# Moving column factors and low halves between VectorE, ScalarE and GpSimd in a hybrid decoder layer

## The chip, the cores and the metric

The kernel runs on one core of a Trainium2 chip. The metric is the device time of one launch in microseconds (us), as the median over runs of the same kernel. Engines: TensorE (PE; PEld is its weight load), VectorE (DVE), ScalarE (ACT), GpSimd (POOL), SyncE (SP, which issues most DMAs).

## The reference

One decoder layer over 2048 tokens of 1024 channels, in float32. The lines that matter:

```python
a = _rmsnorm(h, g_pre_mix[l])
u = jnp.einsum("bsd,dc->bsc", a, w_in[l])          # conv value, conv gate, q, k, v: 5 x 512 columns
conv_out = _conformer_conv(c_val, c_gate, ...)     # GLU, causal depthwise conv of width 31, LayerNorm, swish
attn_out = _stick_breaking(q, k, v)                # 8 heads of 64, no softmax: running products of sigmoids
attn_out = _rmsnorm(attn_out, attn_norm_g[l])
mixed = jnp.concatenate([conv_out, attn_out], axis=-1)
y = jnp.einsum("bsc,cd->bsd", mixed, w_out[l])
h = h + _rmsnorm(y, g_post_mix[l])
f_in = _rmsnorm(h, g_pre_ffn[l])
f = silu(f_in @ w_gate) * (f_in @ w_up) @ w_down   # 2816 hidden channels
h = h + _rmsnorm(f, g_post_ffn[l])
```

`_rmsnorm(x, g)` is `x * rsqrt(mean(x*x) + eps) * g`: a factor for each row (token) and a factor for each channel.

## The kernel before, in words

Tokens are worked on in NG = 4 groups of G = 512 (g = 0 to 3), each of TT = 4 tiles of 128 rows; channels lie in KT = 8 tiles of 128. Activations stand as columns, that is with channels on the partitions and the 512 tokens of a group along the free dimension, so that they can be the moving operand of a matmul with weights as the stationary one.

All large products are made in three parts. An operand x is split in a high half H, its value rounded to the type fp32r, and a low half L = x - H. A product is then L*W_H + H*W_H + H*W_L, three matmuls in fp32r. So each operand costs one pass that rounds (always on ScalarE) and one that subtracts (VectorE or GpSimd). `dense` issues the three matmuls for each channel tile of the input projection (L600, L602, L604), `outproj` those of the output projection (L1043 to L1045), `matmul` (L1117) those of the feed-forward part.

The columns of the first group come from rows that are scaled and turned by TensorE (`scaled`, `to_col`). Those of groups 1 to 3 come from a copy of x that the host has laid out turned: `stats(T)` makes the row factor `rstd1` for 128 tokens; `turned(T)` spreads the four factors of a group over all partitions (`rb`), loads two channel tiles of the turned x into a tile `xcol`, and multiplies each by `rb` on GpSimd (L713). Later `prep(g)` walks over the eight channel tiles: ScalarE multiplies by the channel factor `gpm` and rounds to H (L739), VectorE multiplies by `gpm` again and subtracts H to get L (L740). `xtiles` gives the four tiles that hold H and L of a group, from a pool with two buffers for each kind, which `mixed` shares.

`inproj(g)` computes the 20 blocks of 128 columns for the group. Beside it run three side strands: `attn` (scores L910 and L911, sigmoid `om` L913, running product L916 or L918 on VectorE, transposes L936, their high half TH on ScalarE and low half TL on VectorE in `split` L592 and L593, values L941 and L942), `taps` (the convolution as 31 multiply-adds of 128x512 for each channel tile on VectorE, L826, then a normalization), and `sums` (sums of weight blocks for the feed-forward part on GpSimd, L1201; that part uses Strassen's seven products).

When the conv part (part 0) or the attention part (part 1) of a group is ready, `mixed(g, part)` splits its four channel tiles: H on ScalarE (L873), L on VectorE (L874). `outproj(g, part)` multiplies with w_out, whose own low halves GpSimd makes the first time (`load_w`, L558) and which are read back from memory later. `residual(T)` normalizes the result, adds x and stores the row `hd[T]` together with its factor `rstd2`. `hscaled(T)` loads such a row again and multiplies it by `rstd2` on VectorE (L720); `ffn_in` turns it into columns for the feed-forward part. The rows of the last group are kept and scaled on ScalarE (L1087). `c11` and `p4` are feed-forward products that already run within the mixer; `five` and the loop after it (products b and dps) make the rest.

Two things set the order of the work. The list `PLAN` with the lines `ATTN`, `TAPS` and `SUMS` says in which order the program's instructions are written down: it interleaves main stages and side strands. Then `Graph` takes all instructions up to the end of the last `outproj`, with a cost for each (`cost`, from engine, kind, width, and whether an operand is in PSUM), places them in time under their dependencies and buffers in up to 13 passes forward and backward, and keeps the shortest; `in_order` fixes for each engine the order found. Engines then run in that order and wait for semaphores where data comes from elsewhere. So when an operation changes engine or kind, the order of the mixer on all engines is found anew. After that point the order is the one in which the program is written, in part pinned with `keep_in_program_order`.

Of the kernel before, what the change touches and what calls it, by code (L numbers as in the profile page):

```python
# [10 lines left out]
F32 = mybir.dt.float32  # L11
F32R = mybir.dt.float32r
BF16 = mybir.dt.bfloat16
AF = mybir.ActivationFunctionType
ALU = mybir.AluOpType
# [466 lines left out]
def layer_kernel(ctx: ExitStack, tc: tile.TileContext, x, xT, g_pre_mix, w_in, conv_w, conv_b, ln_g, ln_b,  # L482
                 attn_g, w_out, g_post_mix, g_pre_ffn, w_gate, w_up, w_down, g_post_ffn, out):
    nc = tc.nc
# [13 lines left out]
    rstd2 = cp.tile([P, S // P], F32, name="rstd2")  # L498
# [4 lines left out]
    def const(pool, name, src, shape):  # L503
        t = pool.tile(shape, F32, name=name)
        waiting.append((t, src))
        return t
# [7 lines left out]
    gpm = const(cp, "gpm", g_pre_mix, [P, KT])  # L514

    def bank(name):
        return mm.tile([P, G], F32, tag="mm", name=name)
# [4 lines left out]
    def row(name):  # L522
        return rp.tile([P, D], F32, tag="row", name=name, bufs=4)
# [50 lines left out]
    class Weights:  # L574
# [9 lines left out]
        def next(self):  # L584
            while len(self.tiles) < min(self.n + 1 + self.ahead, len(self.srcs)):
                self.tiles.append(self.load(self.srcs[len(self.tiles)]))
            self.n += 1
            return self.tiles[self.n - 1]
# [109 lines left out]
    def turned(T):  # L698

        g, kp = divmod(T, TT)  # L700
        if kp == 0:
            assert need(*[("stats", g * TT + t) for t in range(TT)])()
            ps = bank("tps")
            for t in range(TT):
                q = g * TT + t
                nc.tensor.transpose(ps[:, t * P:(t + 1) * P], rstd1[:, q:q + 1].to_broadcast([P, P]), id32)
            rb = fup.tile([P, G], F32, tag="rb", name="rb")
            nc.scalar.activation(rb, ps, AF.Copy)
            rbs[g] = rb
        r = row("xcol").rearrange("p (i t) -> p i t", i=2)  # L710
        nc.sync.dma_start(r, xT[g, kp])
        for i in range(2):
            nc.gpsimd.tensor_tensor(r[:, i, :], r[:, i, :], rbs[g], ALU.mult)  # L713
        rows["x", T] = r

    def hscaled(T):
        assert ("h", T) in done
        r = row("hrow")
        nc.sync.dma_start(r, hd[T])
        nc.vector.tensor_scalar(r, r, rstd2[:, T:T + 1], None, ALU.mult)  # L720
        rows["h", T] = r

    def cols(rs, tiles, g, banks=bank):
        for k in range(KT):
            to_col(rs, k, *tiles, g, banks)
            yield 1

    def prep(g):
        xs[g] = xtiles()
        if g == 0:  # L730
            idle = cycle(("z", "at"))
            yield from cols([rows[t] for t in range(TT)], xs[g], gpm,
                            lambda name: pp.tile([P, G], F32, tag=next(idle), name=name))
            return
        Hs, Ls = xs[g]
        for k in range(KT):
            r = rows["x", g * TT + k // 2][:, k % 2, :]
            H = Hs[k // 4][:, k % 4, :]
            nc.scalar.activation(H, r, AF.Copy, scale=gpm[:, k:k + 1])  # L739
            nc.vector.scalar_tensor_tensor(Ls[k // 4][:, k % 4, :], r, gpm[:, k:k + 1], H.bitcast(F32), ALU.mult,  # L740
                                           ALU.subtract)
            yield 1

    def xtiles():
        Hs, Ls = [], []
        for hf in range(2):
            H = xp.tile([P, 4, G], F32R, tag="xH", name="xH", bufs=2)
            L = xp.tile([P, 4, G], F32R, tag="xL", name="xL", bufs=2)
            Hs.append(H)
            Ls.append(L)  # L750
        return Hs, Ls
# [115 lines left out]
    def mixed(g, part, tiles=xtile):  # L867

        yield need(("attn" if part else "conv", g))
        H, L = mc[g, part] = tiles()  # L870
        ms = [ma[g, p] if part else conv[g][:, p, :] for p in range(CB)]
        for k in range(CB):
            nc.scalar.activation(H[:, k, :], ms[k], AF.Copy)  # L873
            nc.vector.tensor_tensor(L[:, k, :], ms[k], H[:, k, :].bitcast(F32), ALU.subtract)  # L874
        if part:
            done.add(("mix", g))
        yield 1
# [406 lines left out]
    def chain(gens):  # L1284
        for gen in gens:
# [3 lines left out]
    taps_s = Side(chain(taps(g) for g in range(NG)), 1 / (NG * (CB * CW + 3 * (TAPLAG + LAG * TT))), ("taps", "conv"))  # L1289
    sums_s = Side(sums(), 1 / (10 * HF))  # L1290
    fns = {"prep": (prep, 8), "qkv": (lambda g: inproj(g, qkv), 12), "gv": (lambda g: inproj(g, gv), 8),
           "in": (lambda g: inproj(g, both), 20),
           "mixc": (lambda g: mixed(g, 0), 1), "outc": (lambda g: outproj(g, 0), 4),
           "mixa": (lambda g: mixed(g, 1), 1), "outa": (lambda g: outproj(g, 1), 4), "fprep": (ffn_in, 8), "c11": (c11, 2 * HF),
           "p4": (p4, 2 * HF)}
    def each(fn):
        def gen(g):
            for t in range(TT):
                fn(g * TT + t)
                yield 1  # L1300
        return gen

    fns["residual"], fns["hscaled"] = (each(residual), TT), (each(hscaled), TT)
    quick = {"scaled": scaled, "stats": stats, "turned": turned, "hscaled": hscaled, "residual": residual,
             "tprep": tprep}
    sides = ((attn_s, ATTN), (taps_s, TAPS), (sums_s, SUMS))
# [32 lines left out]
    with ExitStack() as E:  # L1339
# [13 lines left out]
        for _ in mixed(NG - 1, 1, lambda: operand(*e[0:2])):  # L1353
            pass
# [264 lines left out]
        r = [(R[0], f"t{i}") for i in range(4)]  # L1619
# [77 lines left out]
        for i, (g, n, j) in enumerate(slots):  # L1697
# [9 lines left out]
            if n in (5, 3) and j < TT:  # L1707
                T, r = (TB + j, hrows[j]) if n == 5 else (TA + j, hrows[TT + j])
# [96 lines left out]
```

## Time and profile before

| | |
|---|---|
| median of 3 runs | 2428.36 us (2428.14 to 2428.55) |
| the profiled execution | 2429.93 us, span of its instructions 2428.1 us |
| granted TensorE clock in it, mean | 0.995 |
| PE, DVE, ACT, POOL busy | 2353.6, 1766.3, 1163.8, 1196.0 us |
| the mixer | from 0 to about 1410 us, the rest of the feed-forward part after it |

In the rows of the profile, L and a number is the line of the kernel, then the engine, the operation, the tile written and the tiles read, the shapes, and the count. Times in rows of groups are busy us in all and the mean ns of one, then the idle time of that engine just before them and who ended it. A row of a timeline begins with the start and the duration in us. "PE x L600 <- DVE y L593: 2.9, 5, 1.4" means that PE, before its instructions of line 600 that write x, stood idle for 2.9 us in all, 5 times, 1.4 us at the longest, until VectorE's line 593 had written y.

### The profile page before, as it was taken

To read this page: it belongs to the slowest core of one execution; us is meant where nothing else is said; L and a number is where in the kernel's file an instruction comes from. 1 tells how busy PE (TensorE), PEld (TensorE's weight loads), DVE (VectorE), ACT (ScalarE), POOL (GpSimd) and SP (SyncE) were. 2 spreads that over 40 slices of the span, in tenths; PEclk is the share of its full clock that TensorE was granted. 3 is DMA by queue.
4 is the path that set the end of the run, shared out by engine and by line. 5 is a ranking of instruction groups with operands and counts; after the bars stand their busy time and mean duration, and the time that the engine had idled before them with its cause. 6 is when DMAs were issued, how large, how long until landed. Compare 5 with 4: busy or idle time off the path is not lost. (4 is left out here: it accounts for less than half of the span.)

```text
span 2428.1 us, 33643 instructions
## 1 busy us (share of the span) xinstructions
PE 2353.6 (97%) x11156; PEld 1929.4 (79%) x11156; DVE 1766.3 (73%) x2177; ACT 1163.8 (48%) x2078; POOL 1196.0 (49%) x994
## 2 busy tenths in 40 slices
PE   7999999999999999999999998999999999999998
PEld 5778888788888878887888877777888888887886
DVE  6897899999997799847832357667666664556557
ACT  4346555574555455455564553333232235454443
POOL 5462336422424333428700057755766665467656
PEclk9999999999999999999999999999999999999999
DMA  9888876998688899987897769878888877668765
GB/s 315 266 263 313 259 248 216 308 314 266 223 300 310 264 321 341 314 290 257 266 341 244 272 227 335 310 257 277 295 286 267 271 253 257 196 191 280 236 191 178
DMA packets 283790, 656.67 MB, mean 270 GB/s; under 512 B 34912, under 2 KB 35424, under 8 KB 283616
## 3 DMA queue, kind: packets, MB, share of 16 engines
q1 hardware_dynamic: 267776, 625.68, 77.3%
q10 hardware_dynamic: 15840, 28.84, 3.1%
q8 instruction: 88, 1.44, 0.2%
q14 instruction: 86, 0.70, 0.1%
HBM read 460.40 MB, written 193.99 MB: 270 GB/s over the span
## 5 line engine op out<-in xcount | busy, mean ns | idle before, releaser
L826 DVE SCALAR_TENSOR_TENSOR cv<-glu,cw,cv 128x512 f32<-128x512 f32 x464 | 346.9, 748 | 6.2
L1411 POOL TENSOR_TENSOR wL<-raw,wH 128x512 fp32r<-128x512 f32 x176 | 254.8, 1470 | 194.5 <-ACT wH L1410 163.1
L1642 DVE TENSOR_TENSOR xL__20078<-t__20080,xH__20077 128x512 fp32r<-128x512 f32 x154 | 200.4, 1306 | 159.9 <-ACT xH__20077 L1641 159.8
L1640 POOL TENSOR_TENSOR xL__20076<-t__20079,xH__20075 128x512 fp32r<-128x512 f32 x154 | 212.7, 1388 | 153.6 <-ACT xH__20075 L1639 145.4
L593 DVE TENSOR_TENSOR TL<-at,TH 128x512 fp32r<-128x512 f32 (+1 forms) x320 | 189.5, 601 | 127.7 <-ACT TH L592 117.3
L600 PE MATMUL inps<-xH,wL 128*128 128x512 f32 x640 | 259.4, 406 | 9.9 <-ACT sg L770 8.8
L604 PE MATMUL inps<-xL,wH 128*128 128x512 f32 x640 | 255.7, 401 | 0.6 <-DVE xL L740 0.6
L602 PE MATMUL inps<-xH,wH 128*128 128x512 f32 x640 | 256.3, 401 | 0.0
L1117 PE MATMUL dps<-xL__20076,xH__20077 128*128 128x512 f32 x616 | 240.1, 390 | 2.8 <-POOL xL__20076 L1640 2.8
L1117 PE MATMUL dps<-xH__20075,xL__20078 128*128 128x512 f32 x616 | 240.1, 390 | 2.5 <-DVE xL__20078 L1642 2.1
L1117 PE MATMUL dps<-xH__20075,xH__20077 128*128 128x512 f32 x616 | 239.8, 389 | 0.0
L554 ACT ACTIVATE wH<-raw 128x1024 fp32r<-128x1024 f32 x156 | 165.4, 1061 | 139.9 <-PE inps L604 62.9
L592 ACT ACTIVATE TH<-at 128x512 fp32r<-128x512 f32 (+1 forms) x320 | 168.8, 537 | 130.2 <-PE at L936 113.7
L913 ACT ACTIVATE om<-z 128x512 f32<-128x512 f32 (+2 forms) x320 | 168.8, 542 | 89.3 <-PE z L911 87.8
L1639 ACT ACTIVATE xH__20075<-t__20079 128x512 fp32r<-128x512 f32 x154 | 97.3, 632 | 217.2 <-POOL xL__20076 L1640 121.2
L558 POOL TENSOR_TENSOR wL<-raw,wH 128x1024 fp32r<-128x1024 f32 x50 | 123.1, 2467 | 155.9 <-ACT wH L554 119.3
L936 PE MATMUL at<-idr,om 128*128 128x128 f32 x1088 | 185.4, 273 | 7.2 <-DVE TL L593 2.7
L1410 ACT ACTIVATE wH<-raw 128x512 fp32r<-128x512 f32 x176 | 101.2, 623 | 167.7 <-PE b L1117 49.8
L936 PEld LDWEIGHTS at<-idr,om 128*128 128x128 f32 x1088 | 136.8, 140 | 48.0 <-DVE TL L593 6.3
L1201 POOL TENSOR_TENSOR sum<-sum 128x512 f32<-128x512 f32 x88 | 124.6, 1416 | 100.2 <-DMA sum<-in_w_up_dram 40.3
L918 DVE TENSOR_TENSOR_SCAN om<-om,z 128x512 f32<-128x512 f32 x124 | 156.8, 1271 | 8.5 <-ACT om L913 8.2
L600 PEld LDWEIGHTS inps<-xH,wL 128*128 128x128 f32 x640 | 121.7, 190 | 34.5 <-ACT sg L770 5.8
(296 smaller groups left out, 6103.9 us busy)
## 6 DMA issues: line engine op xcount, KB each, us to landing
wL<-wL SPq DMA_DIRECT2D x156, 512.0 KB, 5.3
raw<-in_w_in_dram SPq DMA_DIRECT2D x80, 512.0 KB, 5.8
t__20080<-u SPq DMA_DIRECT2D x154, 256.0 KB, 2.8
c<-c ACTq DMA_DIRECT2D x88, 256.0 KB, 5.3
t__20079<-wd SPq DMA_DIRECT2D x88, 256.0 KB, 2.9
K<-kd SPq DMA_DIRECT2D x80, 256.0 KB, 4.9
V<-vd SPq DMA_DIRECT2D x80, 256.0 KB, 5.0
u<-accf SPq DMA_DIRECT2D x22, 768.0 KB, 4.6
```

The lines of the kernel that those rows point to most:

```text
L592: nc.scalar.activation(H, ps, AF.Copy)
L593: nc.vector.tensor_tensor(L, ps, H.bitcast(F32), ALU.subtract)
L600: nc.tensor.matmul(ps, WL[:, kc], aH[t](k), start=k == 0, stop=False)
L602: nc.tensor.matmul(ps, WH[:, kc], aH[t](k), start=False, stop=False)
L604: nc.tensor.matmul(ps, WH[:, kc], aL[t](k), start=False, stop=k == KT - 1)
L826: nc.vector.scalar_tensor_tensor(to, gl[c][:, k:k + G], cw[:, c, k:k + 1], a, ALU.mult, ALU.add)
L913: nc.scalar.activation(om[:, 0:w], z[:, 0:w], AF.Sigmoid, scale=-0.125)
L936: nc.tensor.transpose(pt[:, j * P:(j + 1) * P], u["A"][j][:, b * P:(b + 1) * P], id32)
L1117: return nc.tensor.matmul(ps, a, b, skip_group_check=True, **flags)
L1411: nc.gpsimd.tensor_tensor(l, t, f32(h), sub)
L1640: nc.gpsimd.tensor_tensor(WL, w, f32(WH), sub)
L1642: nc.vector.tensor_tensor(UL, t, f32(UH), sub)
```

## The change

Four edits, all before the feed-forward part's second half:

- `turned`: before GpSimd multiplies a channel tile by the row factors, a new pass on ScalarE multiplies it by the channel factor `gpm`, in place (24 passes of 128x512).
- `prep`, groups 1 to 3: the pass that rounds to H no longer multiplies, and L is a plain subtraction on GpSimd in place of the multiply-and-subtract on VectorE (24 times).
- `mixed`: L is subtracted on GpSimd in place of VectorE (32 times, all four groups and both parts).
- `hscaled`: the row of 128x1024 is scaled on ScalarE in place of VectorE (12 times).

```diff
@@ turned
         for i in range(2):
+            nc.scalar.activation(r[:, i, :], r[:, i, :], AF.Copy, scale=gpm[:, 2 * kp + i:2 * kp + i + 1])
             nc.gpsimd.tensor_tensor(r[:, i, :], r[:, i, :], rbs[g], ALU.mult)
@@ hscaled
-        nc.vector.tensor_scalar(r, r, rstd2[:, T:T + 1], None, ALU.mult)
+        nc.scalar.activation(r, r, AF.Copy, scale=rstd2[:, T:T + 1])
@@ prep
-            nc.scalar.activation(H, r, AF.Copy, scale=gpm[:, k:k + 1])
-            nc.vector.scalar_tensor_tensor(Ls[k // 4][:, k % 4, :], r, gpm[:, k:k + 1], H.bitcast(F32), ALU.mult,
-                                           ALU.subtract)
+            nc.scalar.activation(H, r, AF.Copy)
+            nc.gpsimd.tensor_tensor(Ls[k // 4][:, k % 4, :], r, H.bitcast(F32), ALU.subtract)
@@ mixed
-            nc.vector.tensor_tensor(L[:, k, :], ms[k], H[:, k, :].bitcast(F32), ALU.subtract)
+            nc.gpsimd.tensor_tensor(L[:, k, :], ms[k], H[:, k, :].bitcast(F32), ALU.subtract)
```

## The prediction

> **What bounds the kernel now.** I read the page first: the busy shares, the slices, the chain.
>
> ```profile
> span 2428.1 us, 33643 instructions
> PE 2353.6 (97%) x11156; PEld 1929.4 (79%) x11156; DVE 1766.3 (73%) x2177; ACT 1163.8 (48%) x2078; POOL 1196.0 (49%) x994
> PE   7999999999999999999999998999999999999998
> DVE  6897899999997799847832357667666664556557
> POOL 5462336422424333428700057755766665467656
> ```
>
> TensorE is covered nearly everywhere, so only its gaps can be won. VectorE has two lives: in the first 16 slices (971 us, most of the mixer) it stands mostly at 8 or 9 tenths, in the last 16 (from 1457 us, which this change does not edit) at 4 to 7. GpSimd is loose in both, with crowded slices. Next the same by stretches (busy time of PE, PEld, DVE, ACT, POOL, each with its count, then clock, DMA share, GB/s):
>
> ```profile
> 150.00:1000.00 850.00, 833.80 (x4265) 684.57 (x4264) 785.13 (x1081) 472.64 (x850) 321.48 (x322) 1.00 0.86 284
> 1000.00:1390.00 390.00, 386.16 (x1890) 316.16 (x1889) 207.71 (x241) 215.81 (x378) 134.07 (x104) 1.00 0.83 280
> 400.00:440.00 40.00, 39.04 (x181) 30.93 (x180) 39.93 (x53) 18.84 (x30) 29.14 (x26) 1.00 0.76 268
> ```
>
> From 150 to 1000 us PE stands idle 850 - 833.8 = 16.2 us (1.9%) with VectorE busy 92.4%; from 1000 to 1390 us 3.84 us (1.0%) with VectorE at 53%. A busy PE can still be held up, because its matmuls overlap. That shows in the mean of one 128x512 matmul: here the groups of the first stretch, and last the same shape in the down projection (1700 to 2400 us), where VectorE is loose:
>
> ```profile
> L600 PE MATMUL inps<-xH,wL 128*128 128x512 f32 x503 | 202.7, 403 | 3.8 <-ACT sg L770 2.8 <-DVE glu L775 0.5 <-DVE big L1048 0.2
> L604 PE MATMUL inps<-xL,wH 128*128 128x512 f32 x503 | 200.8, 400 | 0.6 <-DVE xL L740 0.6
> L602 PE MATMUL inps<-xH,wH 128*128 128x512 f32 x503 | 200.7, 399 | 0.0
> L910 PE MATMUL z<-K,QL 128*128 128x512 f32 x156 | 65.3, 418 | 1.3 <-DVE om L918 1.3
> L942 PE MATMUL o<-TL,V 128*128 128x512 f32 x155 | 64.4, 415 | 2.2 <-DVE TL L593 2.2
> L1117 PE MATMUL dps<-xH__20075,xL__20078 128*128 128x512 f32 x591 | 230.2, 390 | 1.9 <-DVE xL__20078 L1642 1.5 <-ACT t__20082 L1713 0.4
> ```
>
> The excess over 390 ns is (13 + 10 + 9) x 503 + 28 x 156 + 25 x 155 ns = 24.3 us. It bounds from above what the busy time hides, since part of it is only the change between matmul shapes. So at most 16.2 + 24.3 = 40.5 us are to be won in the stretch where VectorE is full. Who is named for PE's visible gaps from 150 to 1390 us (us in all, times, longest; four largest rows of VectorE, and the largest of ScalarE):
>
> ```profile
> PE o L942 <- DVE TL L593: 2.9, 5, 1.4
> PE inps L600 <- ACT sg L770: 2.8, 2, 1.9
> PE ops L1043 <- DVE vt L593: 1.6, 2, 1.1
> ...
> PE at L936 <- DVE TL L593: 1.6, 3, 0.6
> PE z L910 <- DVE om L918: 1.3, 4, 0.5
> ```
>
> VectorE leads with 7.4 us in these four rows, but no single wait is long: the kernel is bound by PE, with VectorE close behind.
>
> **The change part by part.** What leaves VectorE (the first 1400 us; count, busy us and mean ns of one behind the bar, the idle time before them last), and the four late pieces of the last mixed rows:
>
> ```profile
> L740 DVE SCALAR_TENSOR_TENSOR xL<-xcol,gpm,xH 128x512 fp32r<-128x512 f32 x24 | 22.1, 926 | 0.0
> L874 DVE TENSOR_TENSOR xL<-acc,xH 128x512 fp32r<-128x512 f32 x16 | 12.8, 823 | 5.8 <-ACT xH L873 5.8
> L720 DVE TENSOR_SCALAR hrow<-hrow,rstd 128x1024 f32<-128x1024 f32 x12 | 12.8, 1074 | 0.0
> L874 DVE TENSOR_TENSOR xL<-ma,xH 128x512 fp32r<-128x512 f32 x12 | 11.0, 934 | 1.2 <-PE at L936 1.0 <-ACT xH L873 0.2
> L874 DVE TENSOR_TENSOR e__15143<-ma,e__15142 x4: 683/684/693, 1393.2 to 1398.3; 128x512 fp32r<-128x512 f32 x4
> ```
>
> That is 22.1 + 12.8 + 12.8 + 11.0 + 4 x 0.684 = 61.4 us. Some 44 us of it fall between 150 and 1000 us: all of L740, 16 of the 28 L874 (13.9), 8 of the 12 L720 (8.6). What the other engines do instead is priced by these rows:
>
> ```profile
> L713 POOL TENSOR_TENSOR xcol<-xcol,rb 128x512 f32<-128x512 f32 x24 | 33.4, 1421 | 5.4 <-ACT rb L708 5.4
> L571 POOL TENSOR_TENSOR wL<-raw,wH 128x512 fp32r<-128x512 f32 x22 | 35.1, 1599 | 11.7 <-ACT wH L570 8.6 <-PE z L911 3.2
> L739 ACT ACTIVATE xH<-xcol,gpm 128x512 fp32r<-128x512 f32 x24 | 16.4, 724 | 6.4 <-POOL xcol L713 4.5 <-PE ops L1045 1.3 <-PE inps L602 0.6
> L873 ACT ACTIVATE xH<-acc 128x512 fp32r<-128x512 f32 x16 | 9.3, 626 | 4.4 <-PE c L1117 4.3
> L541 ACT ACTIVATE junk<-big 128x1024 f32<-128x1024 f32 x24 | 25.3, 1057 | 22.6 <-POOL big L1080 16.8 <-DVE big L1048 3.9 <-DVE xL L740 1.8
> ```
>
> GpSimd gains 24 + 32 = 56 subtractions of 128x512, at 1.42 to 1.60 us each: 80 to 90 us more. I take 1.42, the same windows and the same two-input form. ScalarE gains 24 passes with a factor (24 x 0.724 = 17.4), saves the factor in the 24 later ones (24 x 0.098 = 2.4), and takes 12 rows of 1024 at 1.057 to 1.155 (13.9): +28.9 us on the 688 us of both stretches, 4.2%. No DMA changes its queue.
>
> *VectorE's relief.* Between 150 and 1000 us it falls from 785 to 741 of 850 us, its idle time grows from 65 to 109. If PE's idle share there fell to the 1.0% of the loose stretch, 0.9% x 850 = 7.7 us of visible idle would go, and with the hidden part in proportion (40.5 / 16.2 = 2.5) 19 us: the upper end. In proportion to the load, 5.2 of the 39 points between the stretches, it would be 2.6 us; by how much rarer a full VectorE becomes (1 - 65/109 = 0.40), 7.7 us. I take 6, nearer the second, as PE's waits are short waits for a queue that is momentarily full. The lower end is nothing: the window 400 to 440 has VectorE at 39.93 of 40 us and PE at 39.04. What is late next where these waits go is TH and om on ScalarE, and then nothing but PE.
>
> *The low halves come sooner or later?* One op is 0.5 to 0.7 us longer on GpSimd, but on VectorE it stands in line. The third group's columns:
>
> ```profile
> 683.36 1.34 ACT L739 ACTIVATE xH<-xcol,gpm 128x512 fp32r<-128x512 f32 x2
> 684.85 1.34 ACT L739 ACTIVATE xH<-xcol,gpm 128x512 fp32r<-128x512 f32 x2
> ...
> 686.35 0.76 DVE L740 SCALAR_TENSOR_TENSOR xL<-xcol,gpm,xH 128x512 fp32r<-128x512 f32 x1
> 687.01 0.76 DVE L826 SCALAR_TENSOR_TENSOR cv<-glu,cw,cv 128x512 f32<-128x512 f32 x1
> ...
> 694.98 1.71 DVE L740 SCALAR_TENSOR_TENSOR xL<-xcol,gpm,xH 128x512 fp32r<-128x512 f32 x1
> ```
>
> Taps stand between the low halves, and the last ends at 696.7. A free GpSimd starts after the high halves (684.1 for the fifth) and ends four at 1.42 us by about 690. I count -1 us, since the idle of PE at such places is 1 us or less (0.96 in the window 400 to 440). In the loose end, 1000 to 1400 us, the same op is just longer: the last rows' fourth piece would end near 1399.9 instead of 1399.0; PE has the conv half of the output projection as cover. If that cover is gone, it costs 0.9 us; I count 0.
>
> *ScalarE's load.* 4.2% more work before TH and om; against ScalarE's largest PE wait (2.8 us, times 2.5 for the hidden part) that is +0.3 to +0.5 us; I take 0.5. The new pass stands before GpSimd's multiply, so a late column's DMA now stalls ScalarE's line; GpSimd's idle before L713 names no DMA (5.4 us for rb alone), so I count 0 for it, and 2 us if a load is late.
>
> *Sum.* -6 - 1 + 0 + 0.5 = -6.5 us. The profiled execution took 2429.93 us for a span of 2428.1, 1.57 us above the median of 2428.36; taken from the median this gives 2421.9, so 2422 us.
>
> **The rivals.** *The port gives it back (no change).* Rows first: the taps (min/median/max), with one operand in SBUF and one in PSUM, never stretch; an op on SBUF alone does.
>
> ```profile
> L826 DVE SCALAR_TENSOR_TENSOR cv<-glu,cw,cv x464: 723/749/764, 32.0 to 1020.4; 128x512 f32<-128x512 f32 x155
> L740 DVE SCALAR_TENSOR_TENSOR xL<-xcol,gpm,xH x24: 733/754/1755, 167.3 to 695.0; 128x512 fp32r<-128x512 f32 x24
> L916 DVE TENSOR_TENSOR_SCAN om<-lower,om x128: 473/994/3087, 69.7 to 1238.9; 128x128 f32<-128x128 f32 x32, 128x256 f32<-128x256 f32 x32, 128x384 f32<-128x384 f32 x32, 128x512 f32<-128x512 f32 x32
> ```
>
> A stretched op of L740 loses 1.0 us. If each of the 56 new GpSimd passes stretched one of VectorE's remaining SBUF ops (the diagonal scans above all) by that much, 56 us of the 61 us would be given back, and the time stays at 2428, within 2 us. Against it: most of VectorE's ops read PSUM, as the taps do, and do not stretch. The Trainium skill, "SBUF — State Buffer", section "Who interferes with whom", says that a VectorE instruction with two SBUF inputs contends with a GpSimd instruction that reads SBUF, and that whoever loses blocks fully. By that rule the change swaps one contender for another. The trace agrees as to who stretches: 764 ns at most for the taps, 1755 for L740. The same result, 2428, comes if PE alone bounds and its gaps are not VectorE's.
>
> *GpSimd comes late (slower).* Its queue runs in order, and around the second group's columns it is already crowded: 29.14 of the 40 us from 400 to 440. There 8 low halves and two of the mixed rows' are added, 10 x 1.42 = 14.2 us, making 43.3 of 40. From that point on low halves come 3.3 us late, and up to 14 us if the waits in the 10.9 us idle stay in its line. Two such places (this one, and the first group's mixed rows beside the first splitting of the output weights) at 3.3 to 14 us, less half covered by attention, give +3 to +14, middle +8: 2436. It decides when the last low half ends later than VectorE ends it now (435.9 by the second group). For it: the count above. Against it: of GpSimd's 29 us there, 5.6 are weight sums that can move.
>
> **How the numbers follow.** About 0.2% (4.9 us) is what can be told from no change. The forecast, a gain of 5 to 12 us, has 0.40, its own range 2416 to 2423; a larger gain, up to the 19 us of the upper end, 0.08; relief given back or not on the path, with 2424 to 2433, 0.28; GpSimd late, 0.24. So faster 0.48, same 0.28, slower 0.24. The range 2411 to 2434 leaves out the far part of the larger gain and half of the late case, under 2 in 10. The order of all the mixer's instructions is computed anew from the changed list, which shifts every stage a little; that is why the forecast's own range is no narrower.
>
> **What would show it.** Right: VectorE's busy time near 1766 - 61 = 1705 us, with 56 more ops on GpSimd of 1.3 to 1.6 us; PE's idle between 150 and 1000 us at 12 to 14 us instead of 16.2; the mean of L600 and L942 a few ns lower; the last low half of the third group within 6 us of its high half. Wrong by the port: the diagonal scans' mean and maximum up, VectorE's busy time down by 20 us or less. Wrong by GpSimd: PE rows of inps or ops that wait for POOL xL, over 3 us in all. A gain or loss that sits after 1450 us would be none of these, as nothing there is edited.

## The result

The changed kernel takes 2432.3 us against 2428.1 us (medians of 20 runs each): the ratio is 1.0019, 95% interval 1.0012 to 1.0026, so it is slower by about 4.6 us, where 6 us less were forecast. Single executions that took far longer (one of the changed kernel's 20, 4765.6 us) are left out of all ratios. Its profiled execution took 2431.9 us. The rows of the profile below are of one execution of a kernel each.

The first rows of the page after:

```profile
span 2430.1 us, 33665 instructions
PE 2351.1 (97%) x11156; PEld 1925.8 (79%) x11156; DVE 1743.4 (72%) x2109; ACT 1188.7 (49%) x2114; POOL 1255.6 (52%) x1050
```

VectorE is relieved, ScalarE and GpSimd have taken the work, and the span is longer. By stretches (PE, PEld, DVE, ACT, POOL as before), first the kernel before, then the changed one:

```profile
150.00:850.00 700.00, 688.77 (x3527) 567.31 (x3526) 639.94 (x893) 394.08 (x712) 266.25 (x288) 1.00 0.84 275
850.00:1000.00 150.00, 145.03 (x739) 117.26 (x738) 145.19 (x189) 78.56 (x138) 55.23 (x34) 1.00 0.96 329
1000.00:1400.00 400.00, 396.16 (x1936) 324.33 (x1935) 211.38 (x246) 221.85 (x388) 135.91 (x106) 1.00 0.83 282
```

```profile
150.00:850.00 700.00, 693.07 (x3567) 570.95 (x3566) 624.14 (x861) 408.12 (x742) 311.40 (x334) 1.00 0.84 277
850.00:1000.00 150.00, 142.59 (x713) 113.49 (x711) 142.23 (x179) 77.15 (x131) 51.39 (x30) 1.00 0.93 314
1000.00:1400.00 400.00, 388.70 (x1903) 319.51 (x1904) 201.25 (x220) 227.04 (x388) 153.42 (x122) 1.00 0.82 280
```

Up to 850 us PE's idle time falls from 11.2 to 6.9 us. From 850 to 1400 us it rises from 8.8 to 18.7 us (5.0 to 7.4, then 3.8 to 11.3), though VectorE has less to do there. The same in two landmarks, the last matmul of the input projection and the last of the mixer's output projection (the last two numbers ahead of the shape are the first and the last start); first before, then after:

```profile
L604 PE MATMUL inps<-xL,wH x640: 387/389/708, 18.5 to 853.6; 128*128 128x512 f32 x160
L1045 PE MATMUL ops<-wL,e__15142 x32: 387/389/398, 1402.8 to 1424.3; 128*128 128x512 f32 x32
```

```profile
L604 PE MATMUL inps<-xL,wH x640: 387/389/775, 17.9 to 843.2; 128*128 128x512 f32 x160
L1045 PE MATMUL ops<-wL,e__15166 x32: 387/389/397, 1404.4 to 1427.0; 128*128 128x512 f32 x32
```

The input projection ends 10.4 us earlier, the mixer 2.7 us later, with the same matmuls ahead of each landmark (4144 and 4143 of them in the traces up to the first). Of the 10.4 us, 6.7 are idle time of PE up to there (33.7 us before, 27.0 after). Another 3.4 are the granted clock: in the trace of the kernel before it stood at half for 10.2 us in all ahead of that landmark (from 56 and 466 us), after the change for 3.4 us, and one such us costs PE at most half a us. So the relief paid, and 13 us were lost between the two landmarks, 11.0 of them as idle time of PE (8.8 us before, 19.8 after) and none by the clock, which is full there in both. Who is named for PE's gaps from 850 to 1400 us after the change (largest rows; before, no row there exceeds 1.8 us and none names ScalarE for more than 0.4):

```profile
PE o L942 <- DVE TL L593: 3.6, 4, 2.0
PE at L936 <- DVE om L918: 3.1, 3, 1.7
PE c L1117 <- ACT c L1158: 3.0, 2, 1.8
PE o L941 <- ACT TH L592: 2.7, 3, 1.8
PE at L936 <- DVE ot L958: 2.0, 2, 1.2
PE ops L1043 <- ACT c L1158: 1.6, 1, 1.6
```

New are ScalarE's evictions `c` (L1158) of the early feed-forward products. The largest wait of ScalarE for a transfer after the change is of that line. The timeline of the changed kernel, first SyncE's (start, duration, instruction):

```profile
864.01 1.76 SPq L720 DMA_DIRECT2D hrow<-hd  x4
```

Then ScalarE's; the brackets give the idle time before an instruction and what ended it:

```profile
869.07 0.60 ACT L1158 ACTIVATE c<-c 128x512 f32<-128x512 f32 x1 [2.32 <-PE c L1117]
874.69 0.34 ACTq L1123 DMA_DIRECT2D c<-c  x1
875.07 0.60 ACT L1158 ACTIVATE c<-c 128x512 f32<-128x512 f32 x1 [5.40 <-DMA hrow<-hd]
875.57 2.18 ACT L721 ACTIVATE hrow<-hrow,rstd 128x1024 f32<-128x1024 f32 x2
```

And the matmul of PE that stood behind the second eviction:

```profile
875.72 0.50 PE L1117 MATMUL c<-xH,wL 128*128 128x512 f32 x1 [1.25 <-ACT c L1158]
```

ScalarE also issues the stores of these products (L1123, in ScalarE's queue). The first store stands from 869.7 to 874.7 us, until a residual row's load has landed, and the next eviction and everything behind it stand with it.

Why a store waits for another tile's load can be read from the semaphores in the trace. Every transfer, from whichever queue, tells of its landing by one of eight semaphores, which the program uses in turn (259 or 260 times each), and no issue starts before the transfer that had its semaphore last has landed, nearly always the eighth before it (1996 of 2070 times). The store at 874.69 us has the semaphore of the fourth row's load, issued at 865.39 and landed at 874.61. Three issues of SyncE (869.52, 870.98 and 873.37 us) likewise follow the landings of the other three rows (869.51, 870.92 and 873.31 us). So this wait comes from the program. The kernel's reckoning allows for it: `FLIGHT = 8` holds a transfer back until the eighth before it has landed.

### The profile page after: what moved, and what is told of

It reads as the page before. It is cut to its first block, busy times and chain, and to the rows that moved or that the text cites. A ratio compares the mean times of both kernels' runs of the same rounds, so it can differ in the third digit from the quotient of the medians.

```text
span 2430.1 us, 33665 instructions
## 1 busy us (share of the span) xinstructions
PE 2351.1 (97%) x11156; PEld 1925.8 (79%) x11156; DVE 1743.4 (72%) x2109; ACT 1188.7 (49%) x2114; POOL 1255.6 (52%) x1050
## 5 line engine op out<-in xcount | busy, mean ns | idle before, releaser
L600 PE MATMUL inps<-xH,wL 128*128 128x512 f32 x640 | 258.0, 403 | 5.1 <-ACT sg L770 4.8
L1117 PE MATMUL dps<-xH__20099,xL__20102 128*128 128x512 f32 x616 | 240.1, 390 | 3.0 <-DVE xL__20102 L1642 2.3
L1117 PE MATMUL dps<-xL__20100,xH__20101 128*128 128x512 f32 x616 | 240.1, 390 | 1.0 <-POOL xL__20100 L1640 1.0
L1117 PE MATMUL dps<-xH__20099,xH__20101 128*128 128x512 f32 x616 | 239.7, 389 | 0.0
L1201 POOL TENSOR_TENSOR sum<-sum 128x512 f32<-128x512 f32 x88 | 118.1, 1342 | 78.7 <-DMA sum<-in_w_up_dram 33.9
L916 DVE TENSOR_TENSOR_SCAN om<-lower,om 128x128 f32<-128x128 f32 (+3 forms) x128 | 136.6, 1092 | 22.6 <-ACT om L913 22.2
```

The source lines that it names most:

```text
L600: nc.tensor.matmul(ps, WL[:, kc], aH[t](k), start=k == 0, stop=False)
L1117: return nc.tensor.matmul(ps, a, b, skip_group_check=True, **flags)
```

## The experiments

All ratios are to the kernel before, in the same session (its medians there: 2427.3 to 2428.8 us), with 95% intervals.

**One edit at a time.** Theory A was that the relief pays and the rows scaled on ScalarE take it back; B, that the order found anew costs whichever edit changes the list; C, that GpSimd comes late or takes the port.

Only the column edits (`turned` and `prep` as in the change, `mixed` and `hscaled` as before):

> Of the four edits only the two on the next group's columns (factor in an added pass on ScalarE, low half as a plain subtraction on GpSimd); mixed low halves and row scaling stay on VectorE. Theory A (VectorE's relief pays until the input projection ends; the rows scaled on ScalarE, and its stores that wait in line, take it back after 845 us): 4 to 8 us faster than the kernel before (ratio 0.997 to 0.998), and the gain is still there at 1400 us. Theory B (what is lost comes from the order found anew, whichever edit changes the list): anywhere within 5 us of before, with PE's gaps after 845 us as in the changed kernel. Theory C (GpSimd comes late or takes the port): 2 to 4 us slower.

Only `mixed`:

> Only the low halves of the mixed rows go to GpSimd. Theory A: 2 to 5 us faster (23.8 us less on VectorE, ScalarE untouched). Theory B: anywhere within 5 us of before. Theory C: 1 to 4 us slower, with PE waiting for GpSimd's low halves.

Only `hscaled`:

> Only the scaling of the 12 residual rows goes to ScalarE. Theory A: this is the edit that costs: 4 to 8 us slower, lost between 845 and 950 us and between 1100 and 1200 us. Theory B: anywhere within 5 us of before. Theory C: up to 2 us faster, as it frees 12.8 us of VectorE and touches GpSimd nowhere.

All but `hscaled`:

```diff
-        nc.scalar.activation(r, r, AF.Copy, scale=rstd2[:, T:T + 1])
+        nc.vector.tensor_scalar(r, r, rstd2[:, T:T + 1], None, ALU.mult)
```

> The changed kernel with the rows scaled on VectorE again. Theory A: the lead of 9 to 10 us at 845 us is kept, so 6 to 10 us faster than before (ratio 0.996 to 0.9975). Theory B: not faster than before by more than 3 us, since the order is found anew here too and loses elsewhere. Theory C: as slow as the changed kernel or slower, 2432 us and up.

| run | median us | ratio | interval |
|---|---|---|---|
| only columns | 2427.3 | 0.9992 | 0.9982 to 1.0001 |
| only mixed | 2429.8 | 1.0012 | 1.0003 to 1.0022 |
| only row scaling | 2431.9 | 1.0013 | 1.0004 to 1.0022 |
| all but row scaling | 2433.2 | 1.0013 | 1.0004 to 1.0022 |

Theory A falls: without the row scaling the kernel is no faster. No edit by itself is the culprit. Only `mixed` is as slow as theory C expected, but no row of PE's waits from 150 to 1430 us names its low halves on GpSimd in that run. The stretch from 1000 to 1400 us, with only the columns:

```profile
1000.00:1400.00 400.00, 389.74 (x1895) 321.24 (x1894) 210.67 (x239) 218.46 (x375) 130.56 (x103) 1.00 0.83 281
```

With only `mixed`:

```profile
1000.00:1400.00 400.00, 390.79 (x1910) 321.19 (x1909) 208.39 (x229) 220.46 (x382) 150.20 (x118) 1.00 0.81 281
```

With only the row scaling:

```profile
1000.00:1400.00 400.00, 394.03 (x1926) 323.67 (x1925) 210.38 (x245) 225.89 (x388) 133.01 (x105) 1.00 0.81 279
```

With all but the row scaling:

```profile
1000.00:1400.00 400.00, 385.51 (x1876) 315.17 (x1875) 202.76 (x222) 216.06 (x374) 152.79 (x120) 1.00 0.80 274
```

PE is idle there for 10.3, 9.2, 6.0 and 14.5 us, against 3.8 before. The first is telling: the column edits touch nothing after 700 us, and yet 6.4 us are lost after 1000. That is against C as well, and for B.

**Order and engines apart.** `cost` and `Graph` were given a table `AS` of instructions to reckon as another engine's; what runs keeps its real engine, and all other engines keep the order of their instructions:

```diff
-            busy, late = (ISSUE, 0) if dma else cost(i, kind, eng, ins, outs)
+            eng, busy, late = AS.get(i.name) or (eng, *((ISSUE, 0) if dma else cost(i, kind, eng, ins, outs)))
```

The new engines in the old order: `mixed` on GpSimd and `hscaled` on ScalarE, reckoned as VectorE's. The column edits are not in this run, as they add an instruction.

> The mixed rows' low halves on GpSimd and the row scaling on ScalarE, but all instructions in exactly the order of the kernel before: while the order is reckoned, the moved instructions count as VectorE's with VectorE's cost. Theory B (what is lost comes from the order that is found anew): as before, ratio 0.998 to 1.001, because only 36 to 40 us of VectorE's work go elsewhere and PE's order stays. Theory D (the new engines themselves are late in the second half: ScalarE's line, GpSimd's port): slower by 4 us or more, 1.0015 to 1.004, lost after 845 us as in the changed kernel.

The old engines in the new order: all three kinds on VectorE, reckoned as in the changed kernel.

> The converse: exactly the changed kernel's order, reckoned with its engines, but all low halves and the row scaling run on VectorE in it (the added pass with the factor on ScalarE stays). Theory B: as slow as the changed kernel or slower, ratio to before 1.002 to 1.006, and PE loses after 845 us here too, though ScalarE and GpSimd have no more to do there than before. Theory D: the loss after 845 us is gone, ratio 0.998 to 1.001.

The first came out at 2431.4 us, 1.0013 (1.0004 to 1.0022): neither theory's number. The window from 350 to 450 us tells where it lost; in the kernel before:

```profile
350.00:450.00 100.00, 97.10 (x474) 77.91 (x473) 98.66 (x134) 55.73 (x97) 61.34 (x52) 1.00 0.76 256
```

In this run:

```profile
350.00:450.00 100.00, 93.75 (x443) 75.24 (x442) 86.81 (x117) 53.31 (x93) 64.91 (x57) 0.97 0.72 240
```

One of PE's waits there in this run (idle us, count, largest):

```profile
PE ops L1043 <- POOL xL L874: 2.9, 2, 2.1
```

And GpSimd's timeline there in this run:

```profile
356.67 1.30 POOL L874 TENSOR_TENSOR xL<-acc,xH 128x512 fp32r<-128x512 f32 x1
357.92 2.40 POOL L558 TENSOR_TENSOR wL<-raw,wH 128x1024 fp32r<-128x1024 f32 x1
360.26 1.29 POOL L874 TENSOR_TENSOR xL<-acc,xH 128x512 fp32r<-128x512 f32 x1
```

PE waits for low halves on GpSimd, where they stand between the first splittings of the output weights. The other part is the clock: its share is 0.97 in this window against 1.00, because it stood at half for 3.4 us twice, from 363 and from 421 us, which costs PE up to 3.4 us. Whether the waits bring such a spell about no run here isolates. From 1000 to 1400 us this run has PE busy for 396.7 us, as before (396.2): in the old order the new engines cost nothing there, and theory D falls for that stretch.

The second came out at 2461.6 us, 1.0137 (1.0124 to 1.0150), far above what either theory gave. With VectorE's old load the new order is 29 us slower than the changed kernel; PE's row for the low halves TL grew to

```profile
PE o L942 <- DVE TL L593: 17.0, 17, 2.2
```

So the relief is real and large in that order, and the order is made for it.

To see whether the crowded place is all that the new engines cost in the old order, the first group's `mixed` was left on VectorE:

```diff
-            as_(nc.gpsimd.tensor_tensor(L[:, k, :], ms[k], H[:, k, :].bitcast(F32), ALU.subtract), "DVE", 1.04 * G + 500)
+            as_((nc.gpsimd if g else nc.vector).tensor_tensor(L[:, k, :], ms[k], ...), "DVE", 1.04 * G + 500)
```

> As the run with the old order (mixed low halves on GpSimd, row scaling on ScalarE, every instruction in the order of the kernel before), but the first group's mixed low halves stay on VectorE. Theory H (in the old order the new engines cost only at one place, the first group's mixed rows beside the first splitting of the output weights, where GpSimd is crowded): the 4 to 6 us lost between 350 and 450 us come back, ratio 0.997 to 1.000. If GpSimd and ScalarE cost elsewhere too: 1.0005 to 1.002.

Measured: 2427.6 us, 1.0001 (0.9992 to 1.0010), between the two expectations. The medians differ by 3.8 us, the ratios by 0.12%, with intervals that still meet, and in the window PE is busy again for 97.11 us at the full clock:

```profile
350.00:450.00 100.00, 97.11 (x471) 78.03 (x470) 98.20 (x133) 56.21 (x98) 60.22 (x54) 1.00 0.78 263
```

So that place is most of what these two edits cost in the old order, and beyond it they neither cost nor gain within the interval: in an order that was not made for it, VectorE's free time is worth nothing that can be measured. For the column edits this is not shown.

**How much an order matters.** No operation is changed, only the constant HOP of the reckoning:

```diff
-HOP = 60.0
+HOP = 65.0
```

> The kernel before with not one operation changed: only the time that its order reckons for a signal between engines (HOP) is 65 in place of 60 ns, so another order comes out. Theory B: the time moves by 2 to 8 us, up or down, as much as the edits did. Theory D and theory A (an engine's load): within 1.5 us of before.

> The changed kernel with the same different constant, HOP 65. Theory B: moves by 2 to 8 us against the changed kernel, so it can land on either side of the kernel before (2424 to 2438 us). Theories A and D: 2431 to 2434 us, as the changed kernel.

With 65 the kernel before moved by 15 us, more than any theory gave; the changed kernel stayed within 1 us, as A and D expected for it. After these two, theory E was put beside B.

> The kernel before, HOP 55 in place of 60, no operation changed. Theory E (the kernel before owes several us to the order that the constant 60 happens to give it; over other orders the edits gain by VectorE's relief): slower than before by 5 to 15 us, ratio 1.002 to 1.006, as with 65 (1.0068). Theory B alone (orders scatter evenly about the kernel before): as likely 2 to 10 us faster as slower.

> The changed kernel with HOP 55. Theory E: 2426 to 2436 us, and faster than the kernel before with 55 by 4 us or more. Theory B alone: no relation to the kernel before with 55; the two differ by as much either way.

> The kernel before with HOP 70. Theory E: slower than before by 5 to 15 us. Theory B alone: either way.

> The changed kernel with HOP 70. Theory E: 2426 to 2436 us, and faster than the kernel before with 70 by 4 us or more. Theory B alone: either way.

| HOP | before: us, ratio | changed: us, ratio |
|---|---|---|
| 55 | 2447.5, 1.0080 (1.0067 to 1.0092) | 2448.4, 1.0075 (1.0062 to 1.0087) |
| 60 | 2428.1, 1 | 2432.3, 1.0019 (1.0012 to 1.0026) |
| 65 | 2443.3, 1.0068 (1.0053 to 1.0082) | 2431.4, 1.0014 (1.0006 to 1.0023) |
| 70 | 2445.0, 1.0073 (1.0059 to 1.0087) | 2442.5, 1.0057 (1.0045 to 1.0070) |

The order alone moves the time by 15 to 19 us in the kernel before and by up to 17 in the changed one. The first half of E holds: 60 is an outstandingly good value for the kernel before, whose input projection ends 14 to 18 us later with the others. Here with 65:

```profile
L604 PE MATMUL inps<-xL,wH x640: 387/389/776, 16.9 to 867.9; 128*128 128x512 f32 x160
```

And with 55:

```profile
L604 PE MATMUL inps<-xL,wH x640: 387/389/668, 16.7 to 871.1; 128*128 128x512 f32 x160
```

Its second half, a gain of 4 us or more at each other value, holds at 65 only (11.9 us); at 55 and 70 the two differ by less than their intervals, and the changed kernel is slower than the 2426 to 2436 us expected. Over the four values the changed kernel's mean ratio is lower by 0.0014; four values are too few to call that a gain.

An order is paid for in two ways. From 150 us to the end of the mixer, PE's idle time in the kernel before is 10.9, 6.1 and 12.5 us longer with 55, 65 and 70 than with 60. And the clock costs more: it stood at half in spells of 3.4 us or a multiple of that, which cost PE up to 13.6, 8.5 and 11.9 us with 55, 65 and 70, against 1.7 with 60. The third number from the end of this row, with 55, is the clock's share:

```profile
590.00:600.00 10.00, 8.20 (x25) 6.20 (x26) 9.77 (x16) 3.05 (x6) 2.32 (x2) 0.53 0.41 138
```

So in these single executions some half of what the order does to the time comes through the granted clock. What sets off a spell is not shown.

**ScalarE's line.** What in the new order costs after 845 us? The stores of `c11` and `p4` were moved from ScalarE's queue to SyncE's, in exactly the changed kernel's order:

```diff
-        eng.dma_start(stored[key], t)
+        d = (nc.sync if eng is nc.scalar else eng).dma_start(stored[key], t)
+        AS.update({d.ins.name: ("Activation", ISSUE, 0)} if eng is nc.scalar else {})
```

> The changed kernel in exactly its own order, but the 88 stores of c11 and the 22 of p4 are issued by SyncE instead of ScalarE (while the order is reckoned they count as ScalarE's). Theory F (in the new order ScalarE's line stands still while a store waits for an earlier transfer to land, 5.4 us at one place, and that is the loss after 845 us): 3 to 8 us faster than the changed kernel, ratio to before 0.9985 to 1.0005, and PE's waits for ScalarE's c L1158 after 845 us are gone. Theory G (the loss is spread over the new order, above all VectorE's scans; ScalarE's line is one of several): within 2 us of the changed kernel, 1.001 to 1.003.

The control, the same in the kernel before:

> The kernel before in exactly its own order with the same stores issued by SyncE: the control. Theory F: within 2 us of before, as ScalarE stood still for transfers for less there. If it gains as much as the changed kernel does, the stores are no difference between the two; if it loses, SyncE's line is the worse place.

The changed kernel came to 2425.1 us, 0.9996 (0.9987 to 1.0005), a time that theory F expected: 0.23% below its 1.0019, some 5.6 us. At the place shown above the second eviction now waits for PE alone and starts 4.0 us earlier:

```profile
871.04 0.60 ACT L1158 ACTIVATE c<-c 128x512 f32<-128x512 f32 x1 [2.12 <-PE c L1117]
```

The control went the other way, 2431.3 us, 1.0014 (1.0004 to 1.0023): SyncE's line is the worse place in the old order, where one of PE's waits for an eviction grew to 4.1 us. Counting waits over 0.3 us, ScalarE stands before its stores for an earlier landing about as long in the kernel before (12.1 us at eight stores) as in the changed one (12.8 us at nine); what differs is what PE needs from behind them. So ScalarE's stores are a part of the loss that belongs to the new order. Moving them also takes 110 issues of 0.33 us each off ScalarE's line, which this run does not tell apart from the waiting. And it is not all. The stretches of the changed kernel with SyncE's stores:

```profile
850.00:1000.00 150.00, 145.78 (x727) 117.28 (x726) 145.12 (x184) 80.55 (x137) 53.59 (x30) 0.99 0.91 319
1000.00:1400.00 400.00, 391.56 (x1906) 321.21 (x1906) 196.94 (x215) 225.19 (x385) 152.21 (x121) 1.00 0.83 282
```

And PE's waits left in it after 840 us (idle us, count, largest):

```profile
PE o L942 <- DVE TL L593: 3.4, 5, 2.0
PE at L936 <- DVE om L918: 3.1, 3, 1.7
...
PE ops L1043 <- ACT c L1158: 1.6, 1, 1.6
```

PE's idle time from 850 to 1400 us falls from 18.7 to 12.7 us; before it was 8.8. From landmark to landmark this trace takes 579.7 us, against 583.8 in the changed kernel and 570.6 before: two spells at half the clock (from 916 and 1155 us) take back 3.4 us here, and this execution was the slowest of the run's eleven. The row `c L1117 <- ACT c` of 3.0 us fell to 0.4 us or less, the one of `ops L1043` stayed, against the expectation, and VectorE's rows stayed, which were not tried by themselves.

At last the columns alone with SyncE's stores, in the order of the run with the column edits:

> The run with only the column edits, in exactly its order, with the stores of c11 and p4 issued by SyncE. It looks for a version that beats both kernels. Theory F (ScalarE's line behind its stores is the part of the loss that can be taken away): 2 to 5 us faster than the same order with ScalarE's stores, ratio to before 0.9975 to 0.9990. If SyncE's line is as bad a place in this order, as in the order of the kernel before: 0.9990 to 1.0010.

It takes 2425.3 us, 0.9982 (0.9973 to 0.9991): the one version here that is faster than both kernels beyond its interval. PE is busy for 392.6 us from 1000 to 1400 us, against 389.7 with ScalarE's stores; the interval still meets that of the run with ScalarE's stores (0.9982 to 1.0001).

## Why the prediction was wrong

*VectorE's relief* was right in kind and, up to the end of the input projection, in size: PE's idle time fell by 6.7 us there, where 6 + 1 us were reckoned for the whole mixer; the other 3.4 us of the lead are the clock of the two executions. From 150 to 1000 us PE's idle time came to 14.3 us (700 - 693.07 + 150 - 142.59); forecast were 12 to 14. The means of L600 and L942 did not fall: 403 ns as before, and 416 for 415, so nothing of the hidden part, which the upper end multiplied by 2.5, is seen.

*VectorE's busy time* was forecast at 1705 us and is 1743.4. Of the 38 us, 23.5 come with the new order: it has VectorE busy for 1789.8 us in the run that keeps all low halves and the row scaling there. Against that run the move takes off 46.4 us, not 61.4. In part that is because the forecast took durations off a busy time, and instructions that follow each other on VectorE overlap in the profile: added up one by one they last 1885.3 us in the kernel before, of which 1766.3 are busy.

*The port rival* comes close by its signs: VectorE's busy time is down by 22.9 us, where 20 or less were to show it, and the scans are longer in the mean. Here the two rows that most grew, in the first 1400 us of the kernel before:

```profile
L918 DVE TENSOR_TENSOR_SCAN om<-om,one 128x512 f32<-128x512 f32 x44 | 64.9, 1484 | 31.4 <-ACT om L913 31.3
L916 DVE TENSOR_TENSOR_SCAN om<-lower,om 128x512 f32<-128x512 f32 x32 | 45.8, 1430 | 2.3 <-ACT om L913 2.3
```

Of the changed kernel:

```profile
L918 DVE TENSOR_TENSOR_SCAN om<-om,one 128x512 f32<-128x512 f32 x44 | 69.7, 1599 | 32.7 <-ACT om L913 32.6
L916 DVE TENSOR_TENSOR_SCAN om<-lower,om 128x512 f32<-128x512 f32 x32 | 50.1, 1564 | 9.1 <-ACT om L913 9.0
```

And of the run with the new order, but none of the 56 new passes on GpSimd:

```profile
L918 DVE TENSOR_TENSOR_SCAN om<-om,one 128x512 f32<-128x512 f32 x44 | 69.8, 1601 | 30.8 <-ACT om L913 30.8
L916 DVE TENSOR_TENSOR_SCAN om<-lower,om 128x512 f32<-128x512 f32 x32 | 49.9, 1561 | 6.9 <-ACT om L913 6.8
```

So these rows are as long without the new passes: they grew with the order. Over all scans of the execution the sums are 385.6 us before, 399.8 after and 395.4 in that run, so at most 4.4 us of the 14 go with the new passes in this order; in the old order, with `mixed` on GpSimd, the sum is 387.4. That is far from the rival's 56 us. The Trainium skill, "Perfetto Trace Analysis", section "Optimizing Scalar/DVE Operations", warns that moving work between VectorE and GpSimd might not help, as they share an SBUF read port. Here some 49 of the 61 us moved went to GpSimd, and the run with the old engines in the new order, 29 us slower, shows that the move does help where the order uses it.

*The prices* held, on GpSimd at a little less than the 1.42 us taken. Its low halves of the columns, from the groups of the changed kernel:

```profile
L741 POOL TENSOR_TENSOR xL<-xcol,xH 128x512 fp32r<-128x512 f32 x24 | 30.9, 1315 | 0.0
```

And ScalarE's scaled rows by their line (shortest, median and longest in ns; forecast were 1.057 to 1.155 us):

```profile
L721 ACT ACTIVATE hrow<-hrow,rstd x12: 1137/1142/1173, 711.9 to 1175.0; 128x1024 f32<-128x1024 f32 x12
```

*GpSimd comes late* did not happen in the changed kernel: no row of PE's waits from 150 to 1390 us names GpSimd, as the new order leaves room for them. It did happen, at a place that the rival names (the first group's mixed rows), when the old order was kept.

**The step that failed** is the sentence that the order "is computed anew from the changed list, which shifts every stage a little", together with the term for ScalarE. The order was given no term of its own and was left to the forecast's range of 2416 to 2423 us; the runs show 15 to 19 us for another order with no operation changed, and that the kernel before sits at a good value. And the forecast's time was the sum of local prices added to that kernel's order, as if its 3.8 us of idle time from 1000 to 1400 us were a property of a loosely loaded VectorE: the stretch was used as the level to which the tight one could come, and was priced at 0 itself. It rose to 11.3 us. ScalarE's term was set at 0.5 us from its busy time, and at 2 us for a late load; its stores, which stand for earlier landings, were no part of it, and taking all of them off its line gained some 5.6 us in this order. How the rest of the 13 us divides among the small waits for VectorE and ScalarE is not settled.

## What to carry to other kernels

Where one reckoning orders all engines, an edit's price is that of its instructions plus that of a fresh order, and the second can be several times the first: hold the order and change the engines, or vary a harmless constant of the reckoning in both kernels, before an edit is kept or thrown away. Read a lead or a lag at landmarks along the way (the last instruction of a stage), not at the end alone: here +10 and -13 us made -3. A transfer issued from a compute engine's queue is work of that engine: when it has to wait, here for a semaphore that another transfer still holds, all that is behind it waits too. And before a longer row is put down to another engine's new instructions, look at it in a run that has the order without them.

## What was not expected of the hardware

The granted clock is a second price of an order: in these single executions of the kernel before it cost PE up to 1.7 us between 150 us and the end of the mixer with one order and 8.5 to 13.6 us with three others, always as half the clock for 3.4 us or a multiple. A scan over SBUF alone, of 1.25 us at its least, took 1.60 us in the mean in the new order, with the new passes on GpSimd and without them (1.48 in the old one); what lengthens it there is not shown.
